# When the operand pairs of a down projection are made, and in which order its last rows are finished

## The chip, the cores and the metric

The kernel runs on one core of a Trainium2 chip. The metric is the time of one execution on the device, in microseconds (us). An execution has a span, from the start of its first profiled instruction to the end of its last, and a little time around it. The engines are PE (TensorE), with its weight loads (PEld) shown apart, DVE (VectorE), ACT (ScalarE), POOL (GpSimd) and SP (SyncE); in this kernel SP and POOL mainly issue DMAs.

## What is computed

One layer of an encoder: an RMSNorm, a projection, two kinds of token mixing, an output projection, then a SwiGLU feed-forward part and a last RMSNorm. The change touches only the end of it, cut here to what matters:

```python
D_MODEL, SEQ, FFN_HIDDEN = 2048, 512, 5632

h = rmsnorm(x, ffn_norm_w)
x = x + (silu(h @ w_gate) * (h @ w_up)) @ w_down      # w_down: 5632 x 2048
return rmsnorm(x, final_norm_w)
```

All is float32. A product is made of three matmuls of float32r operands: each operand is split into a high part (a rounded copy, made on ACT) and a low part (the rest, a subtraction on DVE), and high by high, high by low and low by high are summed in PSUM.

## The kernel before

The kernel records the work of all engines in program order; each engine then runs its own instructions strictly in the order in which they were recorded, and waits come from buffers. There are two pools of buffers in SBUF, `s2` (62 of 128 x 512, shown as `a` in the profile) and `s4` (20 of 128 x 1024, shown as `b`). A request gets the buffer that has been free longest, so an instruction that fills a buffer waits for the last reader of what lay in it.

The product with `w_down` has three parts. The 44 blocks of 128 rows of `w_down` are numbered in 22 **pairs** of two.

1. Pairs 0 and 1 are multiplied plainly, in four jobs (one for each of four blocks of 512 columns). Their results are added to the residual in DRAM. `before_down` is called ahead of each piece of these jobs, and calls `dn.make(1)` each time.
2. Pairs 2 to 19 are done by the class `Down`, with a seven-product scheme (it needs sums and differences of quarter blocks of both sides). They are cut into three **groups**: the first, X, has pairs 2 to 7; the middle one, Y, has 8 to 14; the third, Z, has 15 to 19. `runs` lists ten runs of (column block, pairs): X for columns 0, 1, 2, then X and Y for column 3, then Y for columns 2, 1, then Y and Z for column 0, and Z for 1, 2, 3. A **piece** is one pair in one run, 7 x 2 x 3 = 42 matmuls (lines 1626 to 1628). There are 72 pieces. I number them from 0: run 0 is pieces 0 to 5, run 3 is pieces 18 to 30, run 6 is pieces 45 to 56, and the last run is pieces 67 to 71.
3. Pairs 20 and 21 are the **tail** (`finish`, lines 1795 to 1797): plain products for four blocks of 128 tokens ("token rows" t = 0 to 3), each with four column blocks, then the residual, the sum of squares, the last norm and the stores.

Two kinds of operand are prepared for a piece.

- The weight side: a piece of `w_down` is loaded by SP (line 1141), summed on DVE (1157 to 1159) and split: two casts on ACT (1169) and two subtractions on DVE (1174). For pieces for which `by_dma` is true, one of the subtractions is done by a DMA that accumulates (ACT 1516 and 1518 and POOL 1517, then ACT 1528 and DVE 1529).
- The activation side: the operands of a pair are made once and kept for all runs that use the pair. The generator `operands` does that in steps; `make(1)` runs one. Step one is four small operations on DVE (1557 to 1560); step two splits the first two operands (ACT 1569 and 1572, DVE 1570 and 1573) and asks SP for the raw block of a later pair (1543); step three splits the other two (ACT 1572, DVE 1573, twice).

`run` records, for each piece i: the sums and splits of the next pieces (up to i + 2), a DMA part for i + 3, then steps of `make`, then the 42 matmuls of i. A guard in `operands` says when a pair may be begun:

```python
if not raws or len(s2.free) < 9 + (raws[0][0] > self.need) * self.reserve:
    yield
    continue
```

`need` is the pair of the current piece and `reserve` is 4, or 11 in runs 4 and 5 and late in run 3. Since `before_down` calls `make`, the first pairs of X are made while the four plain jobs run. Pair 14, the last of Y, is made right ahead of piece 30, which uses it first; the last two steps of pair 19, the last of Z, stand ahead of piece 55, and piece 56 uses it first.

In the tail the loads of the eight weight pieces (`st.load`, line 186) begin ahead of piece 70, their splits (ACT 201, DVE 202) are mostly recorded ahead of piece 71, and the token rows follow one after the other, each with its four column blocks.

## Time and profile before

| | us |
|---|---|
| time, median of 3 runs (2202.18 to 2204.18) | 2203.92 |
| the profiled execution | 2207.85 |
| its span | 2206.1 |
| PE busy within the span | 2180.1 |
| pieces 0 to 71 begin / the tail begins | 1767.63 / 2142.14 |
| last matmul begins | 2196.91 |

The profiled execution is 1.75 us longer than its span and 3.93 us longer than the median. A row of the timeline gives the start, the duration, the engine, the line, the operation and its operands, and in brackets how long the engine sat idle before it and what ended that. Rows of equal instructions that follow each other are merged (x2, x4). Durations overlap a little with the next start, so a rate is read from starts. Times in this document are us from the span's start.

### The profile page before, as it was taken

The page shows a single profiled execution, that of the slowest core. Times are in us where ns is not written, and L with a number is a line of the kernel's source. Part 1 is how long each engine was busy: PE and PEld are TensorE (multiplying, and loading weights), DVE is VectorE, ACT ScalarE, POOL GpSimd, SP SyncE. Part 2 cuts the span into 40 slices and gives each one's busy share as a digit, 9 for nine tenths or more (in the row PEclk, how much of TensorE's full clock was granted, in tenths as well). Part 3 has the DMA queues.
Part 4 walks back from the last instruction along what each step waited for, and adds up shares of the span by engine and source line. Part 5 has one row for each costly group of instructions (what it writes and reads, how often), then busy time and mean ns, then how long its engine had stood idle before and what let it go on. Part 6 is the DMA issues. An engine that isn't in the chain of part 4 may idle for free.

```text
span 2206.1 us, 33648 instructions
## 1 busy us (share of the span) xinstructions
PE 2180.1 (99%) x12594; PEld 1918.7 (87%) x12594; DVE 1589.5 (72%) x2759; ACT 1227.2 (56%) x2038; POOL 327.2 (15%) x361
## 2 busy tenths in 40 slices
PE   9999999999999999999999999999999999999997
PEld 7888888888888888888888888888888899999996
DVE  4366665755556437888888888888888896878886
ACT  5344444444555446666666666666666655545652
POOL 0000000000000101222222222222222212111110
PEclk9999999999999999999999999999999999999998
DMA  6525634222223524889888888898898967767872
GB/s 208 160 84 140 173 92 135 87 93 88 94 86 129 175 98 124 198 194 210 193 209 200 205 206 197 205 201 206 198 204 214 247 187 211 217 187 181 251 255 77
DMA packets 256181, 376.00 MB, mean 170 GB/s; under 512 B 18032, under 2 KB 179488, under 8 KB 256017
## 3 DMA queue, kind: packets, MB, share of 16 engines
q1 hardware_dynamic: 188768, 252.03, 36.6%
q0 software_dynamic: 66064, 120.76, 28.0%
q8 instruction: 99, 1.62, 0.3%
q10 hardware_dynamic: 1184, 1.06, 0.1%
q14 instruction: 66, 0.53, 0.1%
HBM read 246.58 MB, written 35.19 MB: 128 GB/s over the span
## 4 chain that ended last, share of the span: by engine, by line
PE 95%; DVE 2%; DMA 1%; ACT 1%; issue 0%; SPq 0%; DVEq 0%; ACTq 0%
PE pd L1302 22%; PE pd L1308 11%; PE ps L303 5%; PE ps L304 5%; PE ps L305 5%; PE ps L295 5%; PE ps L296 5%; PE ps L297 5%; PE pu L1628 5%; PE pu L1627 5%; PE pu L1626 5%; PE pe L1302 4%; PE pe L1308 2%; PE ps L529 1%; DMA b<-in_w_down_dram 1%; PE ps L537 1%
## 5 line engine op out<-in xcount | busy, mean ns | idle before, releaser
L1302 PE MATMUL pd<-a,b 128*128 128x512 f32 x2112 | 528.6, 392 | 0.8 <-DVE a L1063 0.8
L1302 PEld LDWEIGHTS pd<-a,b 128*128 128x128 f32 x2112 | 379.1, 189 | 66.8 <-DVE a L1063 1.2
L1308 PEld LDWEIGHTS pd<-a,b 128*128 128x128 f32 x2112 | 288.6, 190 | 21.5
L1308 PE MATMUL pd<-a,b 128*128 128x256 f32 x2112 | 295.1, 282 | 0.0
L1628 PE MATMUL pu<-b,a 128*128 128x256 f32 x1008 | 287.4, 285 | 4.7 <-DVE a L1570 4.7
L1626 PE MATMUL pu<-b,a 128*128 128x256 f32 x1008 | 287.4, 285 | 2.4 <-ACT a L1569 2.4
L1627 PE MATMUL pu<-b,a 128*128 128x256 f32 x1008 | 287.3, 285 | 0.3 <-DVE b L1174 0.3
L1209 POOL DMA_DIRECT2D b<-b x176 | 209.8, 1248 | 520.9 <-ACT b L1208 394.1
L202 DVE TENSOR_TENSOR a<-b,a 128x512 fp32r<-128x512 f32 x274 | 184.5, 686 | 133.2 <-ACT a L201 122.1
L1247 ACT CAST b<-b 128x1024 fp32r<-128x1024 f32 x176 | 185.3, 1053 | 166.3 <-DVE b L1233 138.5
L1248 DVE TENSOR_TENSOR b<-b,b 128x1024 fp32r<-128x1024 f32 x176 | 214.9, 1221 | 50.2 <-ACT b L1247 26.3
L1628 PEld LDWEIGHTS pu<-b,a 128*128 128x128 f32 x1008 | 195.2, 194 | 5.1 <-DVE a L1570 5.1
L1626 PEld LDWEIGHTS pu<-b,a 128*128 128x128 f32 x1008 | 195.2, 194 | 2.8 <-ACT a L1569 2.8
L1627 PEld LDWEIGHTS pu<-b,a 128*128 128x128 f32 x1008 | 195.3, 194 | 0.6 <-DVE b L1174 0.5
L201 ACT CAST a<-b 128x512 fp32r<-128x512 f32 x274 | 162.7, 617 | 46.3 <-PE ps L305 22.3
L1330 DVE TENSOR_TENSOR a<-pd,a 128x512 f32<-128x512 f32 x132 | 91.4, 693 | 95.6 <-ACT a L1329 95.6
L1208 ACT ACTIVATE b<-b 128x768 fp32r<-128x768 f32 x176 | 149.2, 848 | 4.7 <-PE ps L305 2.9
L1210 ACT CAST b<-b 128x768 fp32r<-128x768 f32 x176 | 145.3, 825 | 0.6 <-PE ps L305 0.6
L1329 ACT COPY a<-pd 128x512 f32<-128x512 f32 x132 | 77.5, 587 | 102.0 <-PE pd L1308 102.0
L1169 ACT CAST b<-b 128x768 fp32r<-128x768 f32 x92 | 82.3, 942 | 89.3 <-issue 71.7
L1230 DVE TENSOR_TENSOR b<-b 128x512 f32<-128x512 f32 x176 | 120.5, 685 | 0.0
L1174 DVE TENSOR_TENSOR b<-b,b 128x768 fp32r<-128x768 f32 x92 | 98.0, 1088 | 30.3 <-ACT b L1169 26.6
(284 smaller groups left out, 4419.2 us busy)
## 6 DMA issues: line engine op xcount, KB each, us to landing
b<-b POOLq DMA_DIRECT2D x202, 384.0 KB, 5.6
b<-in_w_gate_dram SPq DMA_DIRECT2D x88, 512.0 KB, 4.1
b<-in_w_up_dram SPq DMA_DIRECT2D x88, 512.0 KB, 4.5
b<-in_w_down_dram SPq DMA_DIRECT2D x88, 512.0 KB, 5.7
b<-in_w_in_dram SPq DMA_DIRECT2D x48, 512.0 KB, 4.7
b<-in_w_in_dram SPq DMA_DIRECT2D x94, 256.0 KB, 4.2
b<-in_w_out_dram SPq DMA_DIRECT2D x32, 512.0 KB, 5.4
a<-a SPq DMA_DIRECT2D x96, 128.0 KB, 2.4
```

Of the source, the lines that this page charges most:

```text
L201: act.copy(h[2].t, r)
L202: dve.tensor_tensor(h[3].t, r, h[2].f, op=OP.subtract)
L1208: act.activation(lo.t, r, AF.Copy, scale=-1.0)
L1209: pool.dma_start(out=lo.f, in_=r, accum_op=OP.add)
L1210: act.copy(hi.t, r)
L1247: act.copy(hi.t, self.S[i].t)
L1248: dve.tensor_tensor(lo.t, self.S[i].t, hi.f, op=OP.subtract)
L1302: mm(o, wh.t[:, p, k], x_.t.rearrange("p s t -> p (s t)"), start=first and p == 0, stop=False, skip_group_check=True)
L1308: mm(o[:, 256:512], wl.t[:, p, k], x_.t[:, 0], start=False, stop=last and p == 1, skip_group_check=True)
L1626: mm(o, xh[:, t], wh, start=first and not loaded and h == 0, stop=False, skip_group_check=True)
L1627: mm(o, xh[:, t], wl, start=False, stop=False, skip_group_check=True)
L1628: mm(o, xl[:, t], wh, start=False, stop=last, skip_group_check=True)
```

## The change

It has three parts.

- The guard gets a limit: a pair may be begun only if its number is at most `upto`, and if `gap` buffers of `s2` are free. `upto` begins as 0 and is set in `run`: to the last pair of Y in runs 0 to 5, to the last of Z from run 6 on. `run` makes two steps for each piece in run 3, and one or two in run 6.
- `by_dma` in run 6 holds for the pieces at places 4 to 9 of the run, where it held for 8 to 11.
- The tail: the raw blocks of pairs 20 and 21 are loaded ahead of piece 68, and the residual's rows too; one weight piece is loaded ahead of piece 69 and the limit of four holds from 70 on; token rows 0 and 1 are done together, column by column, and the later splits are spread over their products.

```diff
@@ class Down, __init__
-                self.reserve = self.most = 4
-                self.need = self.pairs[0]
+                self.most, self.upto, self.gap = 4, 0, 13
@@ by_dma
-                return r == 3 or r == 6 and n > 7 or r > 6 and n in (0, 1, 4)
+                return r == 3 or r == 6 and 3 < n < 10 or r > 6 and n in (0, 1, 4)
@@ operands
-                    if not raws or len(s2.free) < 9 + (raws[0][0] > self.need) * self.reserve:
+                    if not raws or raws[0][0] > self.upto or len(s2.free) < self.gap:
@@ run
-                    self.reserve = 11 if r in (4, 5) or r == 3 and n > 6 else 4
-                    self.need = q
+                    self.upto = self.pairs[-1] if r > 5 else self.runs[4][1][-1]
                     while q not in self.x:
                         self.make(1)
-                    self.make((r in (3, 6)) + (i % 2 or r == 3 and n > 6))
+                    self.gap = 10 if r == 6 else 13
+                    self.make(2 if r == 3 else (r == 6) + i % 2)
...
-                    if self.summed(r) and n == len(part) - 2:
+                    if self.summed(r) and n == (1 if r == len(self.runs) - 1 else len(part) - 2):
...
                     if r == len(self.runs) - 1:
-                        if n < 2:
-                            g_load(LAST // 2 + n)
+                        if n == 0:
+                            g_load(LAST // 2)
+                            g_load(LAST // 2 + 1)
                         if n == 1:
+                            st.until, st.limit, st.big = None, 1, tail_first
+                            st.load()
                             g_split(LAST // 2)
                         if n == 2:
                             g_split(LAST // 2 + 1)
-                            st.until, st.limit, st.big = None, 4, tail_first
-                            st.load()
+                            st.limit = 4
+                            st.split(tail_first + 2)
                         if n == 3:
-                            st.split(tail_first + 12)
+                            st.split(tail_first + 8)
@@ finish
-                    if t == 0 and c and k % 2 == 0:
+                    if t < 2 and k % 2:
...
-                for t in range(3):
-                    ys = []
+                for rows in ((0, 1), (2,)):
                     for c in range(4):
-                        b = ps.get()
-                        products(t, c, b, whole)
-                        if t == 0 and c < 3:
+                        for t in rows:
+                            b = ps.get()
+                            products(t, c, b, whole)
                             run_urgent()
-                        residual(c, t, b)
-                        squares(c, t, x1[c], ss2)
-                        ys.append(s2.get())
-                    later(t, ys)
-                    put(*ys, *(x1[c][t] for c in range(4)))
+                            residual(c, t, b)
+                            squares(c, t, x1[c], ss2)
+                    for t in rows:
+                        ys = [s2.get() for _ in range(4)]
+                        later(t, ys)
+                        put(*ys, *(x1[c][t] for c in range(4)))
```

What this does to the engines' orders is shown at three places. In the changed kernel lines 1569 to 1573 are one number lower (1568 to 1572), and the same holds for the other lines of `Down` named above (1515 for 1516, 1527 for 1528). The first place is ACT at the start of `Down`: the last evacuation of the plain jobs (1457), the weight splits of pieces 1 and 2 (four of 1169), and what follows. Before:

```order
L1457 ACTIVATE a_1315_17126<-pu_16_17001,small 128x512
L1169 CAST b_1403_17129<-b_1391_17010 128x768
L1169 CAST b_1404_17131<-b_1396_17069 128x1024
L1169 CAST b_1409_17143<-b_1392_17012 128x768
L1169 CAST b_1410_17145<-b_1402_17101 128x1024
L1169 CAST b_1415_17206<-b_1393_17014 128x768
L1169 CAST b_1416_17208<-b_1408_17139 128x1024
L1569 ACTIVATE a_1316_17216<-b_1389_16948 128x256
L1572 CAST a_1317_17217<-b_1389_16948 128x512
```

The same place on ACT in the changed kernel:

```order
L1457 ACTIVATE a_1268_17005<-pu_16_16909,small 128x512
L1169 CAST b_1398_17008<-b_1387_16912 128x768
L1169 CAST b_1399_17010<-b_1391_16954 128x1024
L1169 CAST b_1404_17022<-b_1388_16914 128x768
L1169 CAST b_1405_17024<-b_1397_16980 128x1024
L1568 ACTIVATE a_1271_17038<-b_1379_16634 128x256
L1571 CAST a_1272_17039<-b_1379_16634 128x512
L1571 CAST a_1274_17041<-a_1269_17032 128x512
L1571 CAST a_1276_17043<-a_1270_17033 128x512
L1169 CAST b_1411_17114<-b_1389_16916 128x768
L1169 CAST b_1412_17116<-b_1403_17018 128x1024
L1568 ACTIVATE a_1280_17124<-b_1380_16636 128x256
```

The raw block `b_1379_16634` is that of pair 2, and `b_1380_16636` that of pair 3. Before, all of pairs 2 to 6 and the first step of pair 7 were recorded within the plain jobs; the pair whose rows stand here (`b_1389`) is pair 7, used first by piece 5. Now no step of any pair is recorded within the jobs. Pair 2 is recorded between the weight splits and piece 0, which uses it, and pair 3 behind the weight split that is recorded for piece 1 and ahead of piece 1, which uses it.

The second place is ACT ahead of piece 30, the last of run 3; 1528 are the weight splits of pieces 29 and 30, 1169 that of piece 31, and 1647 are the evacuations of run 3. Before:

```order
L1528 CAST b_1582_18964<-b_1574_18886 128x1024
L1528 CAST b_1586_19016<-b_1581_18960 128x1024
L1169 CAST b_1590_19068<-b_1571_18827 128x768
L1169 CAST b_1591_19070<-b_1585_19012 128x1024
L1569 ACTIVATE a_1400_19084<-b_1567_18775 128x256
L1572 CAST a_1401_19085<-b_1567_18775 128x512
L1572 CAST a_1403_19087<-a_1398_19078 128x512
L1572 CAST a_1405_19089<-a_1399_19079 128x512
L1647 COPY a_1407_19107<-pu_38_18283 128x512
```

The same place in the changed kernel, where 1568 and 1571 are the last two steps of pair 14:

```order
L1568 ACTIVATE a_1400_18924<-b_1561_18718 128x256
L1571 CAST a_1401_18925<-b_1561_18718 128x512
L1571 CAST a_1403_18927<-a_1398_18861 128x512
L1571 CAST a_1405_18929<-a_1399_18862 128x512
L1527 CAST b_1583_18987<-b_1575_18909 128x1024
L1527 CAST b_1587_19039<-b_1582_18983 128x1024
L1169 CAST b_1591_19091<-b_1572_18850 128x768
```

Pair 14 has moved from behind the split of piece 31 to ahead of the split of piece 29: it is now recorded ahead of piece 27. In run 6 the last step of pair 19 has in the same way moved from ahead of piece 55 to ahead of piece 54, and its two other steps by one and by two pieces.

The third place is DVE in the tail, from the end of the seven-product results (1660, then 1659) to the first sum of squares; 1690 (now 1689) adds their residuals, 1449 is the residual of a tail product, and 202 is half of the split of a tail weight. Before:

```order
L1660 TENSOR_TENSOR b_1860_21858<-a_1538_21850,pu_86_21540 128x2x256
L1690 SCALAR_TENSOR_TENSOR a_1530_21748<-b_1860_21858,small,a_1530_21748 128x512
L1690 SCALAR_TENSOR_TENSOR a_1531_21749<-b_1860_21858,small,a_1531_21749 128x512
L1449 SCALAR_TENSOR_TENSOR a_1487_20755<-pu_87_21909,small,a_1487_20755 128x512
L202 TENSOR_TENSOR b_1862_21929<-b_1854_21820,b_1862_21929 128x512
L202 TENSOR_TENSOR b_1863_21938<-b_1854_21820,b_1863_21938 128x512
```

The same place in the changed kernel:

```order
L1659 TENSOR_TENSOR b_1858_21846<-a_1534_21838,pu_86_21542 128x2x256
L202 TENSOR_TENSOR b_1860_21901<-b_1846_21760,b_1860_21901 128x512
L202 TENSOR_TENSOR b_1861_21910<-b_1846_21760,b_1861_21910 128x512
L1689 SCALAR_TENSOR_TENSOR a_1522_21624<-b_1858_21846,small,a_1522_21624 128x512
L1689 SCALAR_TENSOR_TENSOR a_1523_21625<-b_1858_21846,small,a_1523_21625 128x512
L1449 SCALAR_TENSOR_TENSOR a_1487_20757<-pu_87_21897,small,a_1487_20757 128x512
L202 TENSOR_TENSOR b_1862_21925<-b_1851_21814,b_1862_21925 128x512
L202 TENSOR_TENSOR b_1863_21934<-b_1851_21814,b_1863_21934 128x512
```

Before, twelve of the sixteen halves of the tail's weights were split ahead of these rows and four behind; now eight are split ahead of them and eight behind, two for each of the first four products, and the first eight products alternate between token rows 0 and 1.

## The prediction

> **What bounds the kernel now.** PE is busy for 2180.1 of 2206.1 us, so I ask what PE still waits for, and whether the change adds to it. First the waits of PE from 1700 on (engine, line, releaser: us in total, times, longest).

> ```profile
> PE pu L1628 <- DVE a L1570: 4.7, 2, 2.4
> PE pu L1795 <- ACT b L201: 4.1, 2, 2.7
> ```

> L1570 is the first split of an activation pair, so two stalls are pairs made too late; L1795 is the tail. Now the timeline of the first stall (piece 30, which needs pair 14), engine by engine.

> ```profile
> 1918.30 1.78 ACT L1169 CAST b<-b 128x768 fp32r<-128x768 f32 x2 [3.95 <-PE pu L1628]
> ```

> ```profile
> 1919.17 2.17 DVE L1174 TENSOR_TENSOR b<-b,b 128x768 fp32r<-128x768 f32 x2 [1.91 <-ACT b L1169]
> ...
> 1922.72 0.42 DVE L1570 SCALAR_TENSOR_TENSOR a<-b,a 128x256 fp32r<-128x256 f32 x1
> ```

> ```profile
> 1918.70 0.28 PE L1628 MATMUL pu<-b,a 128*128 128x256 f32 x1
> 1920.45 0.39 PE L1626 MATMUL pu<-b,a 128*128 128x256 f32 x1 [1.47 <-ACT a L1569]
> ...
> 1923.19 0.42 PE L1628 MATMUL pu<-b,a 128*128 128x256 f32 x1 [2.24 <-DVE a L1570]
> ...
> 1926.83 0.29 PE L1627 MATMUL pu<-b,a 128*128 128x256 f32 x1
> ```

> The reader sees a queue. The weight split of piece 31 (two L1169, then two L1174, done 3.0 us after the first began) stands ahead of pair 14 on both engines; the pair's first five operations on DVE take 1.8 us more (1921.34 to 1923.14); PE's third matmul starts 0.05 us after them. The clock comes on top. The windows (busy times and counts of PE, PEld, DVE, ACT, POOL, then PEclk, DMA share, GB/s) show it:

> ```profile
> 1767.60:1797.80 30.20, 30.20 (x253) 30.17 (x252) 29.17 (x46) 18.07 (x27) 4.09 (x7) 1.00 0.69 184
> 1858.30:1908.70 50.40, 50.40 (x422) 50.40 (x421) 43.46 (x77) 35.95 (x54) 10.88 (x15) 1.00 0.99 256
> 1923.20:1926.80 3.60, 3.60 (x17) 3.60 (x18) 3.20 (x6) 1.43 (x3) 0.92 (x2) 0.53 0.60 230
> 2130.00:2140.00 10.00, 9.66 (x81) 9.45 (x80) 6.74 (x10) 2.74 (x5) 0.54 (x1) 1.00 1.03 401
> 2145.00:2147.00 2.00, 0.32 (x2) 0.27 (x2) 1.95 (x5) 1.94 (x4) 0.00 (x0) 1.00 0.36 139
> 2155.50:2165.60 10.10, 8.59 (x19) 5.85 (x19) 6.15 (x12) 3.78 (x11) 0.00 (x0) 0.50 0.01 2
> ```

> At full clock (first row) a matmul takes 0.12 us and a piece of 42 takes 5.04. After the stall 17 matmuls took 3.60 us where 2.04 is normal: 1.6 us more. From 1918.70 to 1926.83 PE started 20 matmuls in 8.13 us, normally 2.40: **the first stall costs 5.7 us**. The second is at piece 56.

> ```profile
> 2053.75 0.84 ACT L1516 ACTIVATE b<-b 128x768 fp32r<-128x768 f32 x1 [2.63 <-DMA b<-in_w_down_dram]
> ```

> ```profile
> 2055.46 0.28 PE L1628 MATMUL pu<-b,a 128*128 128x256 f32 x1
> 2056.63 0.39 PE L1626 MATMUL pu<-b,a 128*128 128x256 f32 x1 [0.89 <-ACT a L1569]
> ...
> 2059.56 0.39 PE L1628 MATMUL pu<-b,a 128*128 128x256 f32 x1 [2.42 <-DVE a L1570]
> ```

> Here ACT waited for a weight load, with pair 19 queued behind it. From 2055.46 to 2059.56 there are 4.1 us where three matmuls take 0.36; with 1.6 for the clock that is **about 5.3 us**.

> **What the change removes there.** Pair 14 now stands ahead of piece 27 and the last step of pair 19 ahead of piece 54, three and two pieces (15.1 and 10.1 us) before their use. The queue at piece 30 (4.8 us to the end of L1570) and the wait of 2.63 us fit in that. What is late next? DVE: in run 3 (second window, pieces 18 to 27) it was busy for 43.46 of 50.40 us with five pairs, and gets a sixth of some 3.7 us: 47.2, so it still keeps up. In run 6 two more pieces (six, not the same ones) have a subtraction made by a DMA, which spares DVE L1174s. I count both stalls as gone: -11.0.

> **What it adds: group X.** In the changed order no pair is begun before `run` sets `upto`. Pairs 2 to 6 and a step of pair 7 leave the plain jobs and stand in run 0, where each pair is behind a weight split and ahead of the piece that uses it. The rows of that place, on ACT, PE and DVE:

> ```profile
> 1768.46 3.46 ACT L1169 CAST b<-b 128x768 fp32r<-128x768 f32 x4
> ...
> 1777.95 1.79 ACT L1169 CAST b<-b 128x768 fp32r<-128x768 f32 x2 [2.43 <-issue]
> 1782.99 1.79 ACT L1169 CAST b<-b 128x768 fp32r<-128x768 f32 x2 [3.25 <-issue]
> ```

> ```profile
> 1767.86 0.28 PE L1628 MATMUL pu<-b,a 128*128 128x256 f32 x1
> ```

> ```profile
> 1773.27 2.09 DVE L1174 TENSOR_TENSOR b<-b,b 128x768 fp32r<-128x768 f32 x2
> ...
> 1787.17 1.28 DVE L1573 TENSOR_TENSOR a<-a,a 128x512 fp32r<-128x512 f32 x2
> ```

> ACT's splits start 5.04 us apart, the length of a piece, and 0.25 us after a piece begins (1767.63 + 2 x 5.04 = 1777.71): they write into buffers that the piece before has just read out. So the split recorded ahead of piece i starts when piece i - 1 ends, and what stands behind it is late.

> - Piece 0: its last weight split ends on DVE at about 1775.2 (the L1174 at 1773.27, a little earlier without the pair steps ahead of it). With 1.8 us for pair 2, PE's third matmul starts at 1777.05 and not at 1767.86: 9.2 us.
> - Pieces 1, 3, 5: L1570 stands right behind the split and ends 0.25 + 3.0 + 0.4 us after the piece was due; the third matmul was due at 0.23. With 0.05 to start, 3.45 each.
> - Pieces 2, 4: the first half of the pair is made a piece earlier, the two L1573 are not. They end 0.25 + 3.0 + 1.3 us after the due time. The third product needs them, and its third matmul is due at 1.67: 2.9 each.

> The sum is 9.2 + 3 x 3.45 + 2 x 2.9 = 25.3 us. The half clock follows each of the six stalls: at 1.6 us each 9.6 more. This is the unknown. Its lower end is 1.6 in all, if only the long stall costs clock (at 2145 nearly 1.7 us of idle time left PEclk at 1.00). Its upper end is 3 us each, 18, because the last window shows 10 us at half clock with gaps inside. I take 9.6, the value of piece 30, whose two gaps are the nearest to these: **+34.9**, between 26.9 and 43.3. Nothing hides it: the first window shows DVE busy for 29.17 of 30.20 us in run 0 already, and PE without a gap to lend.

> [...]

> **The tail.** PE needs for its 16 blocks of 12 matmuls 43.6 us at full clock (0.227 each) and took 54.9 (2142.14 to 2196.91 and one more): 11.3 is the most to be had. DVE sets how much of that comes. Its groups in the tail, and three rows of its timeline, with the ACT row of the splits:

> ```profile
> L1449 DVE SCALAR_TENSOR_TENSOR a<-pu,small,a 128x512 f32<-128x512 f32 x12 | 8.9, 748 | 8.4 <-PE pu L1797 8.4
> L1782 DVE SCALAR_TENSOR_TENSOR a<-a,small,a 128x512 f32<-128x512 f32 x12 | 8.2, 746 | 0.1
> L202 DVE TENSOR_TENSOR b<-b,b 128x512 fp32r<-128x512 f32 x7 | 4.6, 689 | 2.6 <-ACT b L201 2.6
> ```

> ```profile
> 2187.74 0.16 DVE L1778 TENSOR_REDUCE small<-small 128x1 f32<-128x4 f32 x1 [0.79 <-ACT a L409]
> ...
> 2189.37 2.74 DVE L1782 SCALAR_TENSOR_TENSOR a<-a,small,a 128x512 f32<-128x512 f32 x4
> ...
> 2197.51 0.47 DVE L1801 SCALAR_TENSOR_TENSOR a<-pu,small,a 128x256 f32<-128x256 f32 x1
> ```

> ```profile
> 2141.17 3.16 ACT L201 CAST b<-b 128x512 fp32r<-128x512 f32 x5 [0.16 <-DMA b<-in_w_down_dram]
> ```

> The DMA engines were full from 2130 to 2140 (share 1.03). One weight load is recorded a piece sooner, but its buffer is read by the weight split of piece 68; the next ones wait for the splits of 69. So the landings hardly move, and the first eight halves are split at about 2144, four casts of 0.5 us after 2141.17 and one L202.

> [...] Were the engines idle instead, the loads would land up to a piece, 5 us, sooner.

> From 2144 DVE has in order: seven operations on the last results, 0.7 each, 4.9 us; eight L202 at 0.6, 4.8; four L1690 and eight residuals L1449 at 0.7, 8.4; three waits of 1.3 for ACT (two made 2.6 before); a wait of 0.8 and two norms of 4.4 (1.63 of small steps, 2.74 for four L1782), 9.6; row 2's residuals, wait and norm, 8.0; and 5.4 from the end of L1782 (2192.1) to the last L1801. The sum is 45.0, so that L1801 starts near 2189.0, where it was 2197.51: **-8.5**. The ends: -11.3 (PE's loss all gone) and -5 (two more stalls such as the 1.7 us at 2145).

> **Sum.** 34.9 - 11.0 - 8.5 = +15.4 us, made against the profiled execution of 2207.85. That lies 3.9 us above the median of the runs, 2203.92, so on the median I forecast 2219.3.

> **Rivals.**
> - *Free clock* after the five short stalls: 26.9 - 19.5 = +7.4, 2211.3. For it: the idle time at 2145. Against: piece 30. Chance 0.13.
> - *A new wait* for one removed, most likely ACT's L1516 waiting for a load in run 6 (2.63 us before, and more pieces come by DMA): +5.3, 2224.6. Chance 0.11.
> - *Half clock twice as long*: 43.3 - 19.5 = +23.8, 2227.7. For it: 2155 to 2165. Chance 0.08.
> - *Faster*: the splits in run 0 do not hang on PE. Their idle time is put down to "issue", not to PE. If they can begin 3.45 us earlier, the later pairs are made beside PE and only piece 0 pays, 9.2 + 1.6: 10.8 - 19.5 = -8.7, 2195.2. The lead of 3.45 us decides. The rhythm of 5.04 speaks against it. Chance 0.06.
> - *The order does not do what it says*: for group X the recorded rows leave no doubt; that pairs 14 and 19 wait for something else is in the second rival.

> My forecast has 0.62. The range takes in all but the faster case and the outer ends: 2208 to 2230. A measurement tells 0.2% (4.4 us) from no change: faster 0.06, same 0.05 (free clock with all of the tail's 11.3), slower 0.89.

> **What would show it.** In the profile after, PE would stall at each of the first six pieces, released by the pair's splits (L1569 and L1572 in the new numbers), with PEclk well under 1.00 there and piece 0's third matmul near 1777. Pieces 30 and 56 would pass without a stall, and the tail's matmuls would take some 46 us. If PE runs through run 0, the forecast is wrong.

## The result and the profile after

| | before | after |
|---|---|---|
| time, median of 6 runs each (us) | 2204.64 (2202.18 to 2205.76) | 2222.77 (2217.34 to 2224.59) |
| profiled execution, its span | 2207.85, 2206.1 | 2222.80, 2221.0 |
| piece 0 due to piece 6 begins (run 0) | 30.2 | 64.9 (1767.13 to 1831.99) |
| pieces 29 and 30; 55 and 56 | 15.8; 15.4 | 10.08; 10.08 |
| first tail matmul to end of span | 64.0 | 55.7 (2165.28 to 2221.0) |

The ratio is 1.0078, with a 95% interval of 1.0065 to 1.0091. The medians lie 18.1 us apart (the ratio, which goes by the means, gives 17.2), so the changed kernel is slower; +15.4 was forecast. "Due" means the start of piece 0 less PE's wait ahead of it. A piece's length here is read from the start of its first matmul to that of the next piece's.

The waits of PE from 1700 on in the changed kernel (engine, line, releaser: us in total, times, longest). Lines of `Down` are one number lower; the tail's products have moved to L1797 to L1799.

```profile
PE pu L1625 <- ACT a L1568: 11.1, 4, 4.4
PE pu L1627 <- DVE a L1569: 6.0, 4, 4.2
PE pu L1625 <- ACT a L1571: 3.0, 2, 1.5
PE pu L1627 <- DVE a L1572: 1.8, 2, 0.9
PE pu L1797 <- ACT b L201: 1.1, 1, 1.1
PE pu L1798 <- DVE b L202: 0.4, 2, 0.2
```

The four lines at the top are the splits of a pair. All twelve of those waits lie ahead of 1832, two in each of the six pieces of run 0. After that PE waits for no pair any more. The waits for the tail's weights (L201) fell from 4.1 us to 1.1.

The start of run 0 on PE, ACT and DVE (the number in brackets is the engine's idle time ahead of the instruction, with what ended it):

```profile
1771.57 0.39 PE L1625 MATMUL pu<-b,a 128*128 128x256 f32 x1 [4.44 <-ACT a L1568]
1776.28 0.58 PE L1627 MATMUL pu<-b,a 128*128 128x256 f32 x1 [4.21 <-DVE a L1569]
1786.22 0.39 PE L1625 MATMUL pu<-b,a 128*128 128x256 f32 x1 [2.23 <-ACT a L1568]
1787.50 0.39 PE L1627 MATMUL pu<-b,a 128*128 128x256 f32 x1 [0.78 <-DVE a L1569]
1795.88 0.39 PE L1625 MATMUL pu<-b,a 128*128 128x256 f32 x1 [1.52 <-ACT a L1571]
1797.31 0.39 PE L1627 MATMUL pu<-b,a 128*128 128x256 f32 x1 [0.92 <-DVE a L1572]
```

```profile
1784.07 1.78 ACT L1169 CAST b<-b 128x768 fp32r<-128x768 f32 x2 [7.52 <-PE pu L1627]
1785.75 0.41 ACT L1568 ACTIVATE a<-b 128x256 fp32r<-128x256 f32 x1
```

```profile
1784.93 2.17 DVE L1174 TENSOR_TENSOR b<-b,b 128x768 fp32r<-128x768 f32 x2 [3.91 <-ACT b L1169]
1787.02 0.42 DVE L1569 SCALAR_TENSOR_TENSOR a<-b,a 128x256 fp32r<-128x256 f32 x1
```

ACT's weight split at 1784.07 waits 7.52 us for PE, and here the profile names PE as what ended the wait (the last matmul of piece 0 began at 1783.71). The split of pair 3 stands right behind it, on ACT at 1785.75 and on DVE at 1787.02, and PE's first and third matmul of piece 1 (1786.22, 1787.50) start when these two are ready. The rows of pieces 2 to 5 repeat this, the even ones with the second half of a pair. The third matmul of piece 0 starts at 1776.28, where 1777.05 was forecast.

The windows (PE, PEld, DVE, ACT, POOL busy, then PEclk, DMA share, GB/s): run 0; pieces 18 to 27; the tail.

```profile
1767.10:1832.00 64.90, 42.83 (x254) 40.18 (x254) 49.37 (x89) 28.64 (x48) 5.08 (x8) 0.79 0.49 143
```

```profile
1892.40:1942.80 50.40, 50.40 (x422) 50.40 (x422) 45.97 (x85) 37.85 (x58) 10.94 (x15) 1.00 0.99 265
2165.20:2211.60 46.40, 44.87 (x207) 36.46 (x205) 37.89 (x72) 19.65 (x50) 0.00 (x0) 1.00 0.28 102
```

Run 0 needs 49.37 us of DVE where it had 29.17, and PE's clock is at 0.79. In run 3 DVE keeps up with what it got (45.97 us of 50.40, forecast 47.2), and PE has no gap. The tail's matmuls pass at full clock.

### The profile page after: what moved, and what is told of

Its sections match the earlier page's. It is cut to its first block, busy times and chain, and to the rows that moved or that the text cites. A ratio compares the mean times of both kernels' runs of the same rounds, so it can differ in the third digit from the quotient of the medians.

```text
span 2221.0 us, 33659 instructions
## 1 busy us (share of the span) xinstructions
PE 2184.1 (98%) x12594; PEld 1921.2 (87%) x12594; DVE 1587.3 (71%) x2757; ACT 1228.8 (55%) x2040; POOL 329.1 (15%) x363
## 4 chain that ended last, share of the span: by engine, by line
PE 91%; DVE 3%; issue 2%; DMA 1%; ACT 1%; POOL 1%; SPq 0%; DVEq 0%; ACTq 0%; POOLq 0%
PE pd L1302 22%; PE pd L1308 11%; PE ps L303 5%; PE ps L304 5%; PE ps L305 5%; PE ps L295 5%; PE ps L296 5%; PE ps L297 5%; PE pu L1627 5%; PE pu L1626 5%; PE pu L1625 5%; PE pe L1302 4%; PE pe L1308 2%; PE ps L529 1%; PE ps L537 1%
## 5 line engine op out<-in xcount | busy, mean ns | idle before, releaser
L1308 PEld LDWEIGHTS pd<-a,b 128*128 128x128 f32 x2112 | 288.5, 190 | 21.6
L1627 PE MATMUL pu<-b,a 128*128 128x256 f32 x1008 | 290.2, 288 | 7.9 <-DVE a L1569 6.0
L202 DVE TENSOR_TENSOR a<-b,a 128x512 fp32r<-128x512 f32 x273 | 183.3, 686 | 151.6 <-ACT a L201 139.3
L1626 PE MATMUL pu<-b,a 128*128 128x256 f32 x1008 | 289.6, 287 | 0.4 <-DVE b L1174 0.4
L1625 PEld LDWEIGHTS pu<-b,a 128*128 128x128 f32 x1008 | 197.9, 196 | 15.6 <-ACT a L1568 12.2
L1627 PEld LDWEIGHTS pu<-b,a 128*128 128x128 f32 x1008 | 197.9, 196 | 9.5 <-DVE a L1569 7.0
L1626 PEld LDWEIGHTS pu<-b,a 128*128 128x128 f32 x1008 | 197.9, 196 | 0.6 <-DVE b L1174 0.6
L201 ACT CAST a<-b 128x512 fp32r<-128x512 f32 x273 | 161.5, 618 | 46.4 <-PE ps L305 22.3
L1169 ACT CAST b<-b 128x768 fp32r<-128x768 f32 x88 | 78.8, 940 | 99.6 <-issue 77.3
L1174 DVE TENSOR_TENSOR b<-b,b 128x768 fp32r<-128x768 f32 x88 | 94.3, 1090 | 46.2 <-ACT b L1169 42.5
```

What stands on the lines that cost most here:

```text
L201: act.copy(h[2].t, r)
L202: dve.tensor_tensor(h[3].t, r, h[2].f, op=OP.subtract)
L1308: mm(o[:, 256:512], wl.t[:, p, k], x_.t[:, 0], start=False, stop=last and p == 1, skip_group_check=True)
L1625: mm(o, xh[:, t], wh, start=first and not loaded and h == 0, stop=False, skip_group_check=True)
L1626: mm(o, xh[:, t], wl, start=False, stop=False, skip_group_check=True)
L1627: mm(o, xl[:, t], wh, start=False, stop=last, skip_group_check=True)
```

## The experiments

Each ran beside the kernel before on the same chip; a ratio is to that kernel, whose medians were 2205.1 (e1 to e4), 2204.6 (e5 to e8) and 2205.7 (e9 to e11).

### The parts of the change alone

**e1_x_ahead**: the changed kernel, where the limit starts at the last pair of X.

```diff
-                self.most, self.upto, self.gap = 4, 0, 13
+                self.most, self.upto, self.gap = 4, X[-1], 13
```

> The changed kernel with one number altered: the limit `upto` begins at the last pair of X (7), not at 0, so X may again be made during the plain jobs. Theory 'sum': the three parts add up. Run 0 falls back from 64.5 us to 30.2, and the gains stay, 11.0 for pieces 30 and 56 and 8.2 for the tail (the tail's difference between the two profiles): 2204.6 - 19.2 = 2185.4. Rival 'other cause': the loss in run 0 comes from the other new numbers (13 free buffers asked for, two steps in other places), then run 0 stays near 64 us and the time near 2222. Rival 'coupled': the gains were there only because a late start spread the later work; then between 2190 and 2205.

Measured: 2187.95 us, ratio 0.9923 (0.9911 to 0.9936). PE has no wait in run 0, which takes 30.2 us again:

```profile
1767.10:1797.30 30.20, 30.20 (x253) 30.20 (x252) 29.15 (x47) 18.07 (x27) 4.09 (x7) 1.00 0.70 184
```

One number turns the change from 0.8% slower to 0.8% faster. The loss is all in the late group X, and the gains don't hang on it. They are 17.2 us, 2 less than expected, which the interval allows.

**e2_pairs_alone**: the kernel before with the new guard, the new steps of `run` and the new `by_dma`. The limit starts at the last pair of X.

```diff
-                self.reserve = self.most = 4
-                self.need = self.pairs[0]
+                self.most, self.upto, self.gap = 4, X[-1], 13
...
-                return r == 3 or r == 6 and n > 7 or r > 6 and n in (0, 1, 4)
+                return r == 3 or r == 6 and 3 < n < 10 or r > 6 and n in (0, 1, 4)
...
-                    if not raws or len(s2.free) < 9 + (raws[0][0] > self.need) * self.reserve:
+                    if not raws or raws[0][0] > self.upto or len(s2.free) < self.gap:
...
-                    self.reserve = 11 if r in (4, 5) or r == 3 and n > 6 else 4
-                    self.need = q
+                    self.upto = self.pairs[-1] if r > 5 else self.runs[4][1][-1]
...
-                    self.make((r in (3, 6)) + (i % 2 or r == 3 and n > 6))
+                    self.gap = 10 if r == 6 else 13
+                    self.make(2 if r == 3 else (r == 6) + i % 2)
```

> The kernel before with the new guard, the new steps of `run` and the new `by_dma`, X allowed during the plain jobs, and the tail as before. Theory 'sum': pieces 30 and 56 pass without a stall and nothing else moves: 2204.6 - 11.0 = 2193.6. Rival 'new wait' (ACT waits for a load in run 6): one stall is left, 2198.9.

**e3_tail_alone**: the kernel before with the part of the diff that concerns the last run and `finish`, word for word.

> The kernel before with only the last part of the change: loads of the last run and the tail's order. Theory 'sum': the tail from its first matmul to the end of the span takes 55.7 us as in the changed kernel, not 64.0: 2204.6 - 8.2 = 2196.4. Rival: the tail profits from something in the new choice of pieces for the DMA, then 2199 or more.

**e4_x_late**: the kernel before, with X held back.

```diff
+                self.open = False
...
-                    if not raws or len(s2.free) < 9 + (raws[0][0] > self.need) * self.reserve:
+                    if not raws or not self.open or len(s2.free) < 9 + (raws[0][0] > self.need) * self.reserve:
...
+                    self.open = True
```

> The kernel before, where no pair may be begun before `run` begins; all else is as before. Theory 'sum': run 0 takes 64.5 us as in the changed kernel: 2204.6 + 34.2 = 2238.8. Rival 'free clock' (short stalls cost no clock): +25, 2229.6. Rival 'other cause': 2204.6.

Measured: e2 2195.47 (0.9954, 0.9940 to 0.9968), so -9.6; e3 2198.32 (0.9970, 0.9959 to 0.9980), -6.8; e4 2238.30 (1.0152, 1.0134 to 1.0170), +33.2. These differences are in us against the kernel before. Added up they give +16.8; the change itself gave +18.1 by the medians. The three parts are independent within what the runs can tell (e4's interval alone reaches 4 us to each side), and each has the size of its term.

### Why a late group X costs what it costs

The prediction had the pairs late because they stand behind a weight split that waits for PE. A rival is that DVE can't do the work in run 0 at all, wherever it stands.

**e5_pair_first**: the changed kernel, with the missing pair recorded ahead of the splits.

```diff
                     left = len(part) - 1 - n if self.summed(r) else None
+                    self.upto = self.pairs[-1] if r > 5 else self.runs[4][1][-1]
+                    while q not in self.x:
+                        self.make(1)
                     self.load()
...
-                    self.upto = self.pairs[-1] if r > 5 else self.runs[4][1][-1]
-                    while q not in self.x:
-                        self.make(1)
```

> The changed kernel (no pair in the plain jobs), with the loop that makes a missing pair recorded ahead of the weight sums and splits of a piece instead of behind them. Theory 'queue' (the pairs are late only because they stand behind a weight split that hangs on PE): pairs are made while PE still works on the piece before, and run 0 takes little over 30 us: 2190. Rival 'DVE load': sums and splits of a piece take DVE 3.7 us and a pair 3.7, 7.4 in all where PE needs 5.04, and pair 2 comes on top; with all in the best order run 0 still needs some 45 to 48 us: 2204 to 2208. If neither the place in the queue nor the load matters: 2222.

Measured: 2202.11 us (0.9986, 0.9977 to 0.9995), near the rival's 2204 to 2208 and far from the 2190 of "queue". Run 0 takes 44.8 us. Its rows on PE, three on DVE, and the windows of piece 1 and of pieces 2 to 5:

```profile
1777.65 0.39 PE L1627 MATMUL pu<-b,a 128*128 128x256 f32 x1 [3.61 <-DVE a L1569]
1784.78 0.39 PE L1627 MATMUL pu<-b,a 128*128 128x256 f32 x1 [0.21 <-DVE a L1569]
1791.91 0.38 PE L1627 MATMUL pu<-b,a 128*128 128x256 f32 x1 [1.48 <-DVE a L1569]
1799.05 0.39 PE L1627 MATMUL pu<-b,a 128*128 128x256 f32 x1 [1.47 <-DVE a L1569]
```

```profile
1784.31 0.42 DVE L1569 SCALAR_TENSOR_TENSOR a<-b,a 128x256 fp32r<-128x256 f32 x1
...
1791.44 0.42 DVE L1569 SCALAR_TENSOR_TENSOR a<-b,a 128x256 fp32r<-128x256 f32 x1
...
1798.57 0.42 DVE L1569 SCALAR_TENSOR_TENSOR a<-b,a 128x256 fp32r<-128x256 f32 x1
```

```profile
1774.00:1784.20 10.20, 6.59 (x42) 6.37 (x42) 10.03 (x18) 4.32 (x7) 0.00 (x0) 0.83 0.52 155
1784.20:1811.40 27.20, 22.12 (x170) 20.50 (x169) 26.79 (x52) 17.50 (x28) 2.49 (x5) 1.00 0.53 180
```

DVE comes round every 7.13 us without idle time (26.79 us busy of 27.20), and PE follows it. So 20.1 of the 34.6 us were the place in the queue, with the half clock that it brought (PEclk 0.79 over run 0 in the changed kernel, 0.96 in e5), and some 14.5 remain in this order because sums, splits and a pair take DVE longer than the 5.04 us of a piece.

**e6_pair_2_ahead**: the changed kernel with only pair 2 made during the jobs.

```diff
-                self.most, self.upto, self.gap = 4, 0, 13
+                self.most, self.upto, self.gap = 4, X[0], 13
```

> The changed kernel with `upto` beginning at 2: only pair 2 is made during the plain jobs, pairs 3 to 7 as in the changed kernel. Theory 'sum of stalls': the wait ahead of and in piece 0 (4.4 and 4.4 us) and its half clock (some 2 us) go, the five other stalls stay: 2222 - 10 = 2212. Rival 'DVE load': only pair 2's 3.7 us go, 2218.5.

Measured: 2217.66 us (1.0054, 1.0041 to 1.0066): 5.1 less than the changed kernel, not 10, and near the 2218.5 of "DVE load". Piece 0 waits no more, but piece 1 does:

```profile
1773.70 0.39 PE L1625 MATMUL pu<-b,a 128*128 128x256 f32 x1 [2.23 <-ACT a L1568]
1779.26 0.58 PE L1627 MATMUL pu<-b,a 128*128 128x256 f32 x1 [5.05 <-DVE a L1569]
```

The third matmul of piece 1 waits 5.05 us where it waited 0.78. The stalls are not independent. DVE works here from 1767.92 to 1785.05 with no wait, on three weight splits, sums, pair 3 and the first half of pair 4. In the changed kernel part of piece 0's wait had given it time for such work; here it is waited for a piece later.

### The tail: rows or loads

**e7_tail_rows** is e2 with the new loop over `rows` in `finish`, and nothing else of the tail. **e8_tail_loads** is e1 with the old loop `for t in range(3)` put back: earlier loads, eight halves split ahead, rows one after the other.

> The kernel of e2_pairs_alone (2195.5) with token rows 0 and 1 taken together by columns, and loads and splits as before. Theory 'rows': the blocks of columns 2 and 3 come later, so their weight splits are made in time; PE's waits at the fourth block (3.1 and 2.0 us) go with the half clock behind them, only the 2.0 us at the second block stays: 2189. Rival 'loads': the splits come too late because their loads begin late, and rows alone bring nothing: 2195.

> The kernel of e1_x_ahead (2188.0) with the token rows one after the other as before, but its earlier loads and its spread splits. Theory 'rows': eight halves are split late and row 0 needs them sooner, so PE waits again at the columns 2 and 3, at least as long as before: 2195 to 2200. Rival 'loads': the earlier loads carry the gain, 2188 to 2190.

Measured: e7 2188.42 us (0.9925, 0.9912 to 0.9937), e8 2194.82 (0.9959, 0.9946 to 0.9971). The order of the rows carries the whole gain (2195.47 for e2, 2188.42 for e7), the loads and the spread splits alone next to none (2194.82). The wait lines of the two, e7 first:

```profile
PE pu L1794 <- ACT a L1664: 2.0, 1, 2.0
```

```profile
PE pu L1797 <- ACT b L201: 3.8, 2, 2.4
PE pu L1798 <- DVE b L202: 1.8, 2, 1.6
```

Row by row, PE gets to the last column after three blocks and waits for its weights; with two rows at a time it gets there after six. What stays in e7 is one wait of 2.0 us for a copy (L1664) that stands behind twelve casts on ACT. With eight casts ahead (e1) that wait is gone, and one of 1.1 us for the 15th half comes.

**e11_ten_halves** is e1 with ten:

```diff
-                            st.split(tail_first + 8)
+                            st.split(tail_first + 10)
...
-            upto = [first + 8]
+            upto = [first + 10]
```

> The kernel of e1_x_ahead with ten halves of the tail's weights split ahead of the rows, where it has eight (and the kernel of e7_tail_rows twelve). Theory: the wait of PE at the seventh block (1.1 us, for the 15th half) goes because that half is split a block sooner, and the one at the second block (2.0 us in e7, for a copy behind twelve casts on ACT) comes back in part, some 0.9 us for ten: 2187.5 to 2188. Rival: neither shows, 2186.5.

Measured: 2185.77 us (0.9912, 0.9897 to 0.9927), the lowest time of all, though it ran on another chip than e1 and the intervals of the two overlap. It lies below both of my figures: of both waits 0.2 us is left.

```profile
PE pu L1797 <- ACT a L1664: 0.2, 1, 0.2
```

```profile
2130.80:2175.20 44.40, 44.21 (x207) 36.63 (x205) 37.53 (x72) 19.39 (x50) 0.00 (x0) 1.00 0.28 105
```

### The second stall: the pair's place or the DMA's pieces

**e9_pairs_no_dma** is e2 with the old line of `by_dma`. **e10_dma_alone** is the kernel before with the new one.

```diff
-                return r == 3 or r == 6 and n > 7 or r > 6 and n in (0, 1, 4)
+                return r == 3 or r == 6 and 3 < n < 10 or r > 6 and n in (0, 1, 4)
```

> The kernel of e2_pairs_alone without its new choice of pieces for the DMA in run 6. Theory 'order': piece 56 waited because pair 19 stood behind the wait of L1516 for a load; recorded a piece earlier it is no longer caught there, so the stall stays away: 2195.5. Rival 'DMA choice': the new choice moved that wait away from the pair; without it the stall of piece 56 is back: 2195.5 + 5.3 = 2200.8.

> The kernel before with only the new choice of pieces for the DMA in run 6. Theory 'order': pair 19 is still made one piece before its use, behind two splits, and piece 56 stalls as before: 2204.6. Rival 'DMA choice': the stall of piece 56 goes: 2204.6 - 5.3 = 2199.3.

Measured: e9 2199.97 us (0.9972, 0.9963 to 0.9982), e10 2202.60 (0.9987, 0.9979 to 0.9996). Neither theory holds whole. In e9 piece 56 has no stall, as "order" says, yet the time is that of the rival: pieces 52, 57 and 60 take 6.31, 7.39 and 6.17 us, not 5.04, waiting for weight splits on DVE and for copies on ACT (L1598). With piece 59 (5.32) these add 5.0 us.

```profile
PE pu L1626 <- DVE b L1174: 2.2, 3, 1.0
PE pu L1625 <- ACT pu L1598: 1.5, 3, 0.8
```

In e10 pair 19 stands where it stood, and the stall of piece 56 shrinks from 5.3 us to 1.1 (6.13 less 5.04). ACT's rows ahead of it, and PE's third matmul:

```profile
2050.91 0.85 ACT L1516 ACTIVATE b<-b 128x768 fp32r<-128x768 f32 x1 [1.79 <-PE pu L1627]
2051.66 0.82 ACT L1518 CAST b<-b 128x768 fp32r<-128x768 f32 x1
2052.38 1.04 ACT L1528 CAST b<-b 128x1024 fp32r<-128x1024 f32 x1
2053.33 0.41 ACT L1569 ACTIVATE a<-b 128x256 fp32r<-128x256 f32 x1
```

```profile
2056.72 0.39 PE L1628 MATMUL pu<-b,a 128*128 128x256 f32 x1 [0.45 <-DVE a L1570]
```

L1516 no longer waits for a load ahead of the pair. So either edit removes this stall or nearly so, and only the two together leave no other. Its size isn't fixed, though. In the profiles of e3 and e4, whose run 6 is as before, L1516 waits 1.96 and 1.10 us for the load, not 2.63, and the stall is 3.5 and 2.7 us, not 5.3. By the medians e10 gains 3.1 us.

## Why the prediction was right, point by point

- **Group X, forecast +34.9.** In the profile run 0 is 34.6 us longer, and e4, which does only this, costs 33.2. PE's gaps there, taken from the starts of the matmuls less 0.12, are 8.8, 3.3, 2.8, 3.2, 2.8 and 3.2 us: 24.1 where 25.3 was forecast. The rest is 10.5, and the half clock accounts for 10.0 of it (forecast 9.6, see below).
- **The mechanism was half of it.** "The split recorded ahead of piece i starts when piece i - 1 ends, and what stands behind it is late" is what the rows show, and the order as it stands gives those sizes. But it isn't the only limit. DVE's load is the other: e5 takes the queue away and 14.5 us stay. My rival "faster" used a lead on the splits as if DVE were free; with 7.13 us of work for a piece of 5.04 the 10.8 us that it left for run 0 was not to be had this way.
- **The clock, 1.6 us after each stall.** The sum came out, the step didn't, so the sum was luck. The piece 1 waits of 2.23 and 0.78 us cost no clock, and nearly the same waits of piece 3 (2.23 and 0.48) did. In the trace's record of the granted clock, run 0 has not six equal stretches at half clock but four, of 10.24, 6.83, 3.41 and 6.83 us. 97 matmuls started in them and kept PE busy for 21.6 us, where they take 11.6 at full clock (0.12 each): 10.0 more. In e4's profile nearly the same waits (22.1 us in its wait lines, 21.9 here) brought only 17.1 us at half clock, and run 0 took 60.8 us, not 64.9. Neither rival on the clock, free or twice as long (18 us), fits the 10.5. The first row below is pieces 1 and 2 of the changed kernel, the second the start of piece 3, with PEclk third from the end:

```profile
1785.00:1802.00 17.00, 11.38 (x84) 10.36 (x84) 14.55 (x27) 7.36 (x13) 0.00 (x0) 1.00 0.36 124
1802.00:1809.00 7.00, 5.37 (x23) 5.07 (x24) 6.93 (x13) 3.48 (x7) 0.00 (x0) 0.56 0.67 211
```

- **Pieces 30 and 56, forecast -11.0.** In the profile both stalls are gone, 11.05 us; in e2's median -9.6; that the stall of piece 56 was 5.3 us in the profile of before and smaller in two others may be why. For piece 30 the reason given holds (e9, which moves pair 14, has no stall there; e10, which leaves it alone, keeps that stall in full, 6.67 and 9.14 us for pieces 29 and 30). For piece 56 it was incomplete: the new choice of pieces for the DMA, which I noted only as sparing DVE, nearly does it by itself (e10), and without it new waits come up (e9). The rival "a new wait" describes e9, not the change.
- **The tail, forecast -8.5.** The profile shows -8.2, e3's median -6.8 and the step from e2 to e1 -7.5. That landings of the loads would bring little is borne out by e8. "DVE sets how much of that comes" is not. DVE was busy for 37.89 of 46.40 us; three waits of 1.3 us for ACT were forecast, and there they are. The last row is PE's:

```profile
2177.01 1.29 DVE L202 TENSOR_TENSOR b<-b,b 128x512 fp32r<-128x512 f32 x2 [1.30 <-ACT b L201]
...
2181.59 0.69 DVE L202 TENSOR_TENSOR b<-b,b 128x512 fp32r<-128x512 f32 x1 [1.30 <-ACT b L201]
...
2184.85 1.29 DVE L202 TENSOR_TENSOR b<-b,b 128x512 fp32r<-128x512 f32 x2 [1.30 <-ACT b L201]
```

```profile
2184.87 0.50 PE L1797 MATMUL pu<-b,a 128*128 128x512 f32 x1 [1.11 <-ACT b L201]
```

  But PE waited only where the third of them ends, for the same split (1.1 us), and had no wait from 2185.60 to its last matmul. From e1 to e11 the stretch from the first to the last matmul start falls from 45.6 to 44.1 us with the same work on DVE. The reason for the gain is the order: the last column is asked for after six blocks and not after three. PE's own account gives the size: before, it waited 5.9 us in the tail and was busy for 8.7 us at half clock with 18 matmuls, which take 4.1 at full clock (0.227 each), so 4.6 more; in the changed kernel it waits 1.5 us and has no half clock. That is 9.0 us, and the matmul starts of the tail span 8.7 us less. So the forecast followed the wrong engine to nearly the right number, and that was luck.

## What to carry to other kernels

A guard that is to hold work back must be looked at in its first state too: here a limit that starts at 0 kept the pairs out of the plain jobs, where DVE had time to spare (in the 43.7 us ahead of run 0 it was busy for 38.0 us before and for 20.9 in the changed kernel, and PE ran without a gap in both). One number was worth some 34 us. Ahead of a loop in which an engine is full, the question is how much of its work can be done before; moving it about within the loop gave back only the queueing part here (20.1 of 34.6 us). When a result is asked for too soon, changing the order of those who ask (two rows for each column) can do more than preparing it sooner (here 7.1 us, e2 to e7, against 0.7, e2 to e8).

## What was not expected of the hardware

```profile
1782.33:1785.74 3.41, 1.66 (x14) 1.46 (x13) 0.81 (x1) 1.67 (x2) 0.00 (x0) 1.00 0.01 2
1785.74:1789.15 3.41, 2.15 (x14) 1.79 (x14) 3.41 (x6) 2.80 (x7) 0.00 (x0) 1.00 0.52 164
1799.40:1802.81 3.41, 1.52 (x13) 1.32 (x11) 1.75 (x3) 1.81 (x3) 0.00 (x0) 1.00 0.00 0
1802.81:1806.22 3.41, 2.59 (x10) 2.29 (x11) 3.41 (x7) 2.67 (x6) 0.00 (x0) 0.50 0.63 148
```

- The time spreads more. The six runs of the changed kernel lie 7.3 us apart (3.6 before), and the mean clock goes with them: 0.995 in the fastest (2217.34), 0.991 in the slowest (2224.59). In e4 the span of the runs is 10.1 us, 2233.46 to 2243.51. Why the clock differs from run to run was not shown.
